# Context halves of the neighbourhood probabilities turned by DMA, values as half-precision pairs, low parts of the gated branches on VectorE: one core of a two-layer hybrid attention kernel

## The chip, the core and the metric

The kernel runs on one core of a Trainium2 chip. The core's engines work side by side: TensorE (PE) multiplies matrices and transposes by multiplying with an identity, VectorE (DVE) and ScalarE (ACT) work element by element, GpSimd (POOL) does so without reach into PSUM, and SyncE (SP) issues most of the DMAs. Each engine takes its instructions strictly in the order in which the program lists them. The metric is the device time of one execution in microseconds, the median of several runs; smaller is better.

## What is computed

Two layers of a trunk with two parallel attention branches on 512 latent tokens (8 rows of 64 columns) and 256 context tokens, width 1024, 8 heads of 64 channels per branch. Cut to what matters here:

```python
# branch A, per latent query: a window of 8 x 16 neighbours with a bias, and all 256 context keys, one softmax
s_win = einsum(qr, kw) * scale + bias[None]
s_ctx = einsum(qr, kc) * scale
p = softmax(concatenate([s_win, s_ctx]), axis=-1)
a_att = einsum(p[..., :128], vw) + einsum(p[..., 128:], vc)
# branch B: grouped queries (8 query heads, 2 key heads) over latent and context keys
b_att = attend(q, k_all, v_all)
# merge
o_a = (a_att * silu(a_z)) @ w_o_a
o_b = (b_att * silu(b_z)) @ w_o_b
out = (sigmoid(g_a) * o_a + sigmoid(g_b) * o_b) @ w_out
x = x + gate_x * out
```

In layer 0 the context tokens are queries as well (they attend to the context alone) and are updated in the same way; layer 1 returns the latent tokens.

## The kernel before

Everything is float32 in and out. A product of float32 matrices is made of three PE passes: each operand is split into a high part that PE takes at full speed and a low part, the rest (`mm3`, L433 to L435). Weights arrive by DMA on SP (`raw`, 3 buffers, L401 and L415), ACT casts the high part (`whi`, L403 and L418) and DVE or POOL subtracts for the low part (`wlo`, L406 and L420), with 8 buffers each.

A layer runs through these stages; times are those of the profiled execution.

1. Keys, values and queries of branch A. `evac_va` (L551) takes each of the six value tiles from PSUM: ACT writes the high part and DVE the low part, both float32, into two large tiles `va0` and `va1`.
2. The neighbourhood stage (160 to 295 us in layer 0, 768 to 882 us in layer 1): `pipeline` goes over the 8 heads, emits the scores of head h, then the values of head h-1, then a share of `fill`, the gate projections that have nothing to do with attention and keep PE at work. `na_scores` makes four score tiles of 128 queries by 512 keys: 256 window keys and the 256 context keys. For each, DVE adds the bias and finds the maximum (L958), ACT takes the exponential with its sum (L961), DVE inverts the sum (L762), and the tile is scaled, on DVE for two of the four (L765) and on POOL for the other two (L767, L768). `na_values` turns the probabilities so that keys lie on partitions: `transpose_split` lets PE transpose four 128 by 128 blocks into one PSUM tile (L777, L779), ACT copies the high part (L785) and DVE subtracts the low part (L786). A head takes four such rounds, two for the context half (used by L981, L982) and two for the window half (L986 to L992). In layer 0 the 256 context queries of a head take a fifth (`ctx_scores`, `ctx_values`, L905 and L906). `head_out` adds the two halves of the result (L795, L796) and multiplies it onto the gate (L797).
3. Keys, values and queries of branch B (295 to 385 us in layer 0).
4. The grouped-query stage (385 to 556 us, 940 to 1062 us). Here the probabilities are turned by DMA already: `turned` lets ACT write a 16-bit copy (L802) and DVE or POOL the 16-bit rest (L803), and one DMA on SP (L804) transposes both into `ht`. The values of this branch are 16-bit pairs, scaled to a known range by `shrink`, and `divide` puts the softmax sum and the scale back. While this stage runs, `prepare` splits branch A's gated result into high parts (`gah`, ACT, L656) and low parts (`gal`, POOL, L657), and `early` does so for three quarters of branch B's (`gbh`, `gbl`).
5. The output projections, the merge and the residual.

Large intermediate tiles come from one pool of nine (`big`). In layer 0 a background list (`gate_steps`) makes the output gate from `w_ada`: 8 weight tiles per half, each loaded by SP (L288) and multiplied with two vectors by DVE (L295). Half 0 runs beside the last heads of the neighbourhood stage, half 1 beside the grouped-query stage. The program is written head by head, and a list scheduler then fixes the order of the instructions on each engine; it decides which fill matmul stands between which parts of a head.

Of the kernel before, what the change touches and what calls it, by code (L numbers as in the profile page):

```python
# [7 lines left out]
F32 = mybir.dt.float32  # L8
# [17 lines left out]
NP_NA = (7, 8)  # L26
# [6 lines left out]
NA_POOL = (1, 3)  # L33
# [37 lines left out]
def hybrid_kernel(es: ExitStack, tc, x, ctx, cvec, w_ada, w_ada0, small, gvec, w_in, w_o_a, w_o_b, w_out,  # L71
# [482 lines left out]
    def split_v(ps, hi, lo, hi_src=None):  # L554
        S.copy(R(hi), ps)
        V.tensor_tensor(R(lo), ps, hi, ALU.subtract)

    def evac_va(dsts):
        def f(t, ps):
            d = dsts[t // 3].rearrange("p (t n) -> p t n", t=3)[:, t % 3, :]  # L560
            d = d.rearrange("p (r q d) -> p r q d", q=4, d=64)
            s = ps.rearrange("p (r e d) -> p r e d", e=2, d=64)
            hi, lo = d[:, :, 0:4:3, :], d[:, :, 1:3, :]
            split_v(s, hi, lo)
        return f
# [18 lines left out]
    def layer(l, hx, nxt, start):  # L584
# [144 lines left out]
        va = [big("va0"), big("va1")]  # L729
        w = load_w(W, C_AV, 512, KT, mix_lo)  # L730
        for t in range(6):
            tok_proj(w, 512, a_hx, t, evac_va(va))
# [16 lines left out]
        for t in range(qt):  # L749
            tok_proj(w, 512, a_hx, t, evac_na(qav, True, gq, YB if first else 4))  # L750
            run(bg, per_bg)
# [7 lines left out]
        if True:  # L759
            def softmax_tail(p, n, r, pieces, eng=None):  # L760

                V.reciprocal(r, r)  # L762
                for i, (c0, c1) in enumerate(pieces):
                    if eng is None:
                        V.tensor_scalar(p[:, c0:c1], p[:, c0:c1], r[:, i:i + 1], 0.5, ALU.mult, ALU.mult)  # L765
                    else:
                        G.tensor_scalar(r[:, i:i + 1], r[:, i:i + 1], 0.5, None, ALU.mult)  # L767
                        G.tensor_tensor(p[:, c0:c1], p[:, c0:c1],  # L768
                                        r[:, i:i + 1].to_broadcast([128, c1 - c0]), ALU.mult)

            def transpose_split(blocks, n0=0, n1=512):
# [8 lines left out]
                if att["spare"]:  # L780
                    hi, lo = R(p_tile()[:, 0:512]), R(p_tile()[:, 0:512])
                else:
                    hi = att["p"].tile([128, 512], F32R, tag="pth", name=nm("pth"), bufs=att["nt"])
                    lo = att["p"].tile([128, 512], F32R, tag="ptl", name=nm("ptl"), bufs=att["nt"])
# [715 lines left out]
```

## Time and profile before

| what | value |
|---|---|
| median of 3 runs | 1125.91 us (1125.44 to 1126.06) |
| profiled execution | 1127.56 us |
| its span, first to last instruction | 1125.6 us |
| mean granted PE clock | 0.993 |
| TensorE busy | 1093.3 us, 97% |
| VectorE busy | 774.7 us, 69% |
| ScalarE busy | 579.0 us, 51% |
| GpSimd busy | 490.6 us, 44% |

In a row of a stage table the pairs are busy microseconds and, in brackets, the number of instructions; PEld is the loading of weights into the array, which overlaps the matmuls; PEclk is the share of the clock that PE was granted. In a row of a group stand line, engine, operation, output and inputs with their shapes and the count, then busy microseconds and the mean nanoseconds of one, then the idle time just before and what ended it. In a row of the timeline stand start, duration, engine, line and operation, and in square brackets the idle time before it with its releaser. Matmul durations reach from issue to a modelled end and overlap one another; the distance between two starts is what one of them costs. A row for a tile or line gives the shortest, median and longest duration in nanoseconds.

### The profile page before, as it was taken

What the parts mean: (1) busy time and instruction counts of PE and PEld (TensorE: products, weight loads), DVE (VectorE), ACT (ScalarE), POOL (GpSimd) and SP (SyncE); (2) the same over time, 40 slices, a digit from 0 to 9 for tenths busy, and PEclk for the clock granted to TensorE, in tenths of its full rate; (3) what the DMA queues carried; (4) which work ended last, traced back from release to release, by engine and by line L of the source; (5) the groups of instructions that cost most, each with busy time, mean ns of one, the idle gap of its engine ahead of it and who ended that gap; (6) DMA issues with size and microseconds to landing.
All of it is one profiled execution on the core that took longest, in us unless ns stands there. A gap on an engine that the chain in (4) does not pass through costs nothing.

```text
span 1125.6 us, 16862 instructions
## 1 busy us (share of the span) xinstructions
PE 1093.3 (97%) x5826; PEld 905.3 (80%) x5826; DVE 774.7 (69%) x1492; ACT 579.0 (51%) x1154; POOL 490.6 (44%) x405
## 2 busy tenths in 40 slices
PE   8999999999999999979999999999999999999998
PEld 5688888888998877757788888888888987776677
DVE  4666788897466477776577785458878765677473
ACT  6453266665433576755330284326666446776431
POOL 1054254654247144454521545235554563563531
PEclk9999999999999999989999999999999999999999
DMA  9454322242351488869633532553333236989742
GB/s 373 143 172 140 114 63 66 73 136 89 93 168 38 123 201 185 185 172 269 173 108 125 183 129 72 142 174 92 100 107 116 59 105 172 188 224 239 197 145 80
DMA packets 192222, 161.29 MB, mean 143 GB/s; under 512 B 116364, under 2 KB 158088, under 8 KB 190472
## 3 DMA queue, kind: packets, MB, share of 16 engines
q1 hardware_dynamic: 184800, 145.82, 46.8%
q0 software_dynamic: 2368, 7.87, 2.1%
q10 hardware_dynamic: 4968, 6.53, 1.7%
q8 instruction: 46, 0.75, 0.3%
q14 instruction: 40, 0.33, 0.1%
HBM read 115.58 MB, written 17.32 MB: 118 GB/s over the span
## 4 chain that ended last, share of the span: by engine, by line
PE 38%; issue 4%; DVE 3%; DMA 3%; POOL 2%; ACT 1%; SPq 1%; POOLq 0%; ACTq 0%
PE psx L435 6%; PE psx L433 6%; PE psx L434 6%; PE psf L433 4%; PE psf L434 4%; PE psf L435 4%; PE pss L955 1%; PE pss L861 1%; POOL wlo L406 1%; PE pss L862 1%; PE pst L779 1%; PE pst L1148 1%; DMA raw<-in_w_o_a_dram 1%; PE pst L1149 1%; DMA raw<-in_w_in_dram 1%
## 5 line engine op out<-in xcount | busy, mean ns | idle before, releaser
L420 POOL TENSOR_TENSOR wlo<-raw,whi 128x512 fp32r<-128x512 f32 x70 | 97.9, 1405 | 106.1 <-ACT whi L418 70.4
L433 PE MATMUL psf<-hx,whi 128*128 128x512 f32 (+1 forms) x360 | 138.0, 383 | 3.2 <-ACT zt L614 2.4
L435 PE MATMUL psf<-hx,wlo 128*128 128x512 f32 (+1 forms) x360 | 135.8, 377 | 0.0
L434 PE MATMUL psf<-hx,whi 128*128 128x512 f32 (+1 forms) x360 | 135.1, 375 | 0.0
L433 PE MATMUL psx<-whi,hx 128*128 128x512 f32 (+1 forms) x328 | 120.8, 372 | 0.0
L434 PE MATMUL psx<-wlo,hx 128*128 128x512 f32 (+1 forms) x328 | 119.6, 366 | 0.0
L435 PE MATMUL psx<-whi,hx 128*128 128x512 f32 (+1 forms) x328 | 119.5, 365 | 0.0
L418 ACT CAST whi<-raw 128x512 fp32r<-128x512 f32 x136 | 82.3, 620 | 64.0 <-DMA raw<-in_w_in_dram 35.3
L406 POOL TENSOR_TENSOR wlo<-raw,whi 128x512 fp32r<-128x512 f32 x40 | 61.2, 1535 | 122.1 <-ACT whi L403 80.1
L803 POOL TENSOR_TENSOR h<-p,h 128x768 f16<-128x768 f32 (+1 forms) x40 | 65.7, 1644 | 96.4 <-ACT h L802 72.0
L403 ACT CAST whi<-raw 128x512 fp32r<-128x512 f32 x88 | 54.1, 623 | 99.2 <-PE psx L435 34.2
L420 DVE TENSOR_TENSOR wlo<-raw,whi 128x512 fp32r<-128x512 f32 x66 | 73.6, 1115 | 30.6 <-ACT whi L418 29.0
L504 POOL TENSOR_TENSOR ss<-ss,ehalf 128x8 f32<-128x8 f32 (+2 forms) x40 | 62.5, 1566 | 72.9 <-DVE ss L501 72.8
L433 PEld LDWEIGHTS psf<-hx,whi 128*128 128x128 f32 x360 | 67.9, 188 | 15.4 <-ACT zt L614 3.7
L435 PEld LDWEIGHTS psf<-hx,wlo 128*128 128x128 f32 x360 | 67.8, 188 | 11.6
L1131 DVE CUSTOM_DVE_ANT_0 p<-pss,vb 128x768 f32<-128x768 f32 x64 | 60.3, 953 | 23.6 <-PE pss L862 21.1
L434 PEld LDWEIGHTS psf<-hx,whi 128*128 128x128 f32 x360 | 67.9, 189 | 10.3
L1132 ACT ACTIVATE p<-pss,mx 128x768 f32<-128x768 f32 x64 | 57.6, 900 | 34.7 <-DVE mx L1131 33.7
L435 PEld LDWEIGHTS psx<-whi,hx 128*128 128x128 f32 x328 | 61.9, 189 | 10.0
L434 PEld LDWEIGHTS psx<-wlo,hx 128*128 128x128 f32 x328 | 62.0, 189 | 9.2
L433 PEld LDWEIGHTS psx<-whi,hx 128*128 128x128 f32 x328 | 61.8, 189 | 8.9
L435 PE MATMUL psx<-hx,wlo 128*128 128x256 f32 (+1 forms) x208 | 68.0, 327 | 0.0
(362 smaller groups left out, 3095.8 us busy)
## 6 DMA issues: line engine op xcount, KB each, us to landing
raw<-in_w_in_dram SPq DMA_DIRECT2D x168, 256.0 KB, 2.9
rawb<-in_w_ada_dram SPq DMA_DIRECT2D x48, 256.0 KB, 2.8
raw<-in_w_out_dram SPq DMA_DIRECT2D x32, 256.0 KB, 2.9
tg<-gs SPq DMA_DIRECT2D x4, 1536.0 KB, 6.8
rawx<-in_w_ada_dram SPq DMA_DIRECT2D x4, 1024.0 KB, 9.8
rawy<-in_w_ada_dram SPq DMA_DIRECT2D x4, 1024.0 KB, 9.5
gs<-zt ACTq DMA_DIRECT2D x16, 256.0 KB, 2.0
raw<-in_w_o_a_dram SPq DMA_DIRECT2D x16, 256.0 KB, 3.4
```

What stands on the lines that cost most here:

```text
L403: S.copy(hi[:, :n], raw[:, :n])
L406: e.tensor_tensor(lo[:, :n], raw[:, :n], F(hi[:, :n]), ALU.subtract)
L418: S.copy(hi, raw)
L420: lo_eng(i).tensor_tensor(lo, raw, F(hi), ALU.subtract)
L433: T.matmul(ps, lhs[0], rhs[0], start=first, stop=False)
L434: T.matmul(ps, lhs[0], rhs[1], start=False, stop=False)
L435: T.matmul(ps, lhs[1], rhs[0], start=False, stop=last)
L504: G.tensor_tensor(ss, ss, ehalf[:, :n], ALU.pow)
L779: T.transpose(pt[:, c0:c0 + 128], src, ident)
L803: eng.tensor_tensor(h[:, 1], p[:, :n], h[:, 0], ALU.subtract)
L1131: V.tensor_tensor_reduce(p, pss, lift, -1.0, 3e38, ALU.add, ALU.min, mx[:, 0:1])
L1132: S.activation(p, pss, AF.Exp, bias=mx[:, 0:1], accum_out=r[:, i:i + 1])
```

## The change

**Values of branch A.** `evac_va` now only copies the tile to float32 (`vf`), takes absolute values on ACT and their maximum on DVE. `split_va`, after the first query tile, finds the largest maximum (`shrink`, with one transposition and one small matmul on PE), and `halves` writes scaled 16-bit pairs in three passes on ACT and three on DVE. `head_out` multiplies the scale back in its two existing operations.

**Context half.** The two context rounds of `transpose_split` in `na_values` go. `na_scores` calls `turned` for each tile's 256 context columns: an ACT cast, a POOL subtraction and a DMA transposition (two, of 64 partitions each, for the edge tile), which land in `ht`, one more large tile with a half for even and one for odd heads. In layer 0 the context queries go the same way (`hc`, 512 columns). The context matmuls come first in a head's accumulation, so a head's values begin when its transpositions have landed.

**Scaling.** The two tiles that POOL scaled are scaled by ACT, after one more DVE multiplication of the 128 inverted sums.

**Window half.** Still transposed on PE; both parts are now 16-bit, side by side in one tile.

**Low parts of the gated branches.** `prepare` and `early` give `hilo` DVE in place of POOL.

**Other places.** Half 0 of layer 0's `gate_steps` moves from the neighbourhood stage to stage 3. Branch B's values keep two slots instead of three, and their size is found by absolute values. Layer 0 gets 8 probability buffers instead of 7.

```diff
-NP_NA = (7, 8)
+NP_NA = (8, 8)
+NH_NA = 4
-NA_POOL = (1, 3)
+NA_ACT = (1, 3)
+P_UP = 2.0 ** 14
...
+    def size(v, junk, mx):
+        S.activation(junk, v, AF.Abs)
+        V.tensor_reduce(mx, junk, AX, ALU.max)
...
+    def halves(v, d, s):
+        S.activation(d[:, :, 0, :], v, AF.Copy, scale=s)
+        V.scalar_tensor_tensor(d[:, :, 1, :], v, s, d[:, :, 0, :], ALU.mult, ALU.subtract)
...
-            hilo(za, gated["a"], range(4))
+            hilo(za, gated["a"], range(4), V)
...
+        def evac_va(t, ps):
+            S.copy(vf[:, t, :], ps)
+            size(ps, vab[:, 512 * t:512 * t + 512], vmx[:, t:t + 1])
+        def split_va():
+            V.tensor_reduce(vmx[:, 6:7], vmx[:, 0:6], AX, ALU.max)
+            shrink(vmx[:, 6:7], vsa, vsa[0:1, 2:3], 0.5 / P_UP)
+            for t in range(0, 6, 2):
+                halves(vf[:, t:t + 2, :].rearrange("p t (h d) -> p (t h) d", d=64),
+                       va[:, t:t + 2].rearrange("p t h q d -> p (t h) q d"), vsa[:, 0:1])
...
+                if on_act:
+                    V.tensor_scalar(r, r, P_UP, None, ALU.mult)
                 for i, (c0, c1) in enumerate(pieces):
-                    if eng is None:
-                        V.tensor_scalar(p[:, c0:c1], p[:, c0:c1], r[:, i:i + 1], 0.5, ALU.mult, ALU.mult)
+                    if on_act:
+                        S.activation(p[:, c0:c1], p[:, c0:c1], AF.Copy, scale=r[:, i:i + 1])
                     else:
-                        G.tensor_scalar(r[:, i:i + 1], r[:, i:i + 1], 0.5, None, ALU.mult)
-                        G.tensor_tensor(p[:, c0:c1], p[:, c0:c1],
-                                        r[:, i:i + 1].to_broadcast([128, c1 - c0]), ALU.mult)
+                        V.tensor_scalar(p[:, c0:c1], p[:, c0:c1], r[:, i:i + 1], P_UP, ALU.mult, ALU.mult)
...
+            turns = big("ht").bitcast(F16)
...
+                    at = [(0, 64, 0), (448, 512, 64)] if i == 0 else [(128 * i - 64, 128 * i + 64, 0)]
+                    turned(p[:, 256:512], 256, [(ht[:, :, a:b], n, n + b - a) for a, b, n in at], G)
...
                 for k in range(2):
-                    c0 = 256 + 128 * k
-                    hi, lo = transpose_split(
-                        [(pe[:, c0:c0 + 128], None)]
-                        + [(pp[:, c0:c0 + 128], 64 + 128 * i) for i, pp in enumerate((p0, p1, p2))])
-                    T.matmul(po, vsl(4 + k), hi, start=k == 0, stop=False)
-                    T.matmul(po, vsl(4 + k), lo, start=False, stop=False)
+                    for a in range(2):
+                        T.matmul(po, vsl(4 + k), ht[:, 2 * a + k, :], start=k + a == 0, stop=False)
...
-            bg = gate_steps((0,), att["p"]) if first else []
-            pipeline(fill, 9, na_first, values_of(za, na_values), bg=bg)
+            bg = []
+            pipeline(fill, 9, na_first, values_of(za, na_values, vsa[:, 1:2], False), bg=bg)
...
-            bg = []
+            bg = gate_steps((0,), hp["p"]) if first else []
             w = load_w2(W, C_BKV, KT, mix_lo)
...
-                hilo(zb, gated["b"], range(3))
+                hilo(zb, gated["b"], range(3), V)
```

What the scheduler makes of it is seen in the order of the instructions. On PE, the values of layer 0's first neighbourhood head (`psv`; `pth` and `ptl` are the turned context halves, `pst` the PSUM tiles of the window's transposes) stood before the change so:

```order
L982 MATMUL psv_1671<-ptl_1678,va_116_712 128x512
L981 MATMUL psv_1671<-pth_1688,va_116_712 128x512
L777 MATMUL pst_1694<-ident,p_1473 128x2x64
L779 MATMUL pst_1694<-ident,p_1483 128x128 x2
L982 MATMUL psv_1671<-ptl_1689,va_116_712 128x512
L779 MATMUL pst_1694<-ident,p_1494 128x128
L777 MATMUL pst_1707<-ident,p_1473 128x2x64
L779 MATMUL pst_1707<-ident,p_1494 128x128
L779 MATMUL pst_1707<-ident,p_1504 128x128 x2
```

and now, at the same place, the context matmuls read what the DMA turned (`ht`), behind the first scores of the next head (L972), and the window's parts (`pt`) follow; the weights of 16-bit matmuls are listed as rows of their own:

```order
L972 MATMUL pss_1885<-kh_1476,qs_1862 128x512
L972 MATMUL pss_1885<-kl_1477,qs_1862 128x512
L996 LDWEIGHTS va_712
L996 MATMUL psv_1736<-ht_1475,va_712 128x512
L996 LDWEIGHTS va_712
L996 MATMUL psv_1736<-ht_1475,va_712 128x512
L996 LDWEIGHTS va_712
L996 MATMUL psv_1736<-ht_1475,va_712 128x512
L996 LDWEIGHTS va_712
L996 MATMUL psv_1736<-ht_1475,va_712 128x512
L1000 LDWEIGHTS va_712
L1000 MATMUL psv_1736<-pt_1746,va_712 128x192
```

The four context matmuls now stand together, with no transpose of their own before them.

On POOL, in layer 0's grouped-query stage, the low parts of branch A (`gal`) stood before the change as one row of four between two weight subtractions:

```order
L797 TENSOR_TENSOR zb_4086<-zb_4086,ho_5477 64x512
L420 TENSOR_TENSOR wlo_5512<-raw_5508,whi_5510 128x512
L657 TENSOR_TENSOR gal_5328<-za_1045,gah_5327 128x768 x4
L420 TENSOR_TENSOR wlo_5690<-raw_5686,whi_5688 128x512
L797 TENSOR_TENSOR zb_4086<-zb_4086,ho_5490 64x256
```

and now they stand on DVE (L666), among a later head's work (L897 is a score maximum, L848 the multiplication by the inverted sums, L1147 the next head's first maximum):

```order
L823 TENSOR_TENSOR ho_5434<-pst_5421,ho_5434 64x512
L666 TENSOR_TENSOR gal_5285<-za_1053,gah_5284 128x768
L897 TENSOR_REDUCE mx_5403<-pss_5398 128x2
L666 TENSOR_TENSOR gal_5285<-za_1053,gah_5284 128x768 x2
L899 TENSOR_SCALAR mx_5403<-mx_5403 128x2
L848 SCALAR_TENSOR_TENSOR zb_4043<-pst_5592,vb_3395,zb_4043 64x512
L666 TENSOR_TENSOR gal_5285<-za_1053,gah_5284 128x768
L422 TENSOR_TENSOR wlo_5475<-raw_5471,whi_5473 128x512
L1147 ISA p_5529,mx_5530<-pss_5524,vb_3395 128x768
```

The train of four left POOL and is spread over DVE's row with two or three instructions of the heads between its parts.

On SP, in layer 0's neighbourhood stage, weights (`raw`), gate weights (`rawb`) and bias tiles (`bint`, `bedg`) followed each other before the change:

```order
L935 DMA bedg_1448<-in_bias_edge_dram 64x128 x2
L415 DMA raw_2716<-in_w_in_dram 128x2x256
L288 DMA rawb_2589<-in_w_ada_dram 128x512
L933 DMA bint_1447<-in_bias_int_dram 128x256
L415 DMA raw_2722<-in_w_in_dram 128x2x256
L415 DMA raw_2988<-in_w_in_dram 128x2x256
```

and now weights and bias tiles share the queue with the transpositions (L840):

```order
L417 DMA raw_2298<-in_w_in_dram 128x2x256
L840 DMA_TRANSPOSE ht_1475<-h_1896 128x4x128
L840 DMA_TRANSPOSE ht_1475<-h_1910 128x4x128
L840 DMA_TRANSPOSE ht_1475<-hc_1943 128x8x128
L840 DMA_TRANSPOSE ht_1475<-h_1925 128x4x128
L840 DMA_TRANSPOSE ht_1475<-h_2119 128x4x64 x2
L840 DMA_TRANSPOSE ht_1475<-h_2135 128x4x128
L947 DMA bint_1469<-in_bias_int_dram 128x256
L949 DMA bedg_1470<-in_bias_edge_dram 64x128 x2
```

A head brings six transpositions to this queue in layer 0 and five in layer 1, and a bias or weight load behind one of them waits for the cast and the subtraction that it waits for.

More of the change, by code (lines that the diff above doesn't have):

```diff
@@ L552, in evac_na, with shrink @@
         return f
[L554 to L565, printed above, removed]
+    def size(v, junk, mx):
+        S.activation(junk, v, AF.Abs)
+        V.tensor_reduce(mx, junk, AX, ALU.max)
+    def shrink(mx, s, row, post):
+        pt = psw(512, "t")
+        T.transpose(pt[0:1, 0:128], mx, ident)
+        V.tensor_reduce(row, pt[0:1, 0:128], AX, ALU.max)
+        T.matmul(pt[:, 128:129], row.to_broadcast([1, 128]), ident[0:1, 0:1], start=True, stop=True)
+        V.tensor_scalar(s[:, 1:2], pt[:, 128:129], 1.0e-30, 1.0 / V_UP, ALU.max, ALU.mult)
+        V.reciprocal(s[:, 0:1], s[:, 1:2])
+        V.tensor_scalar(s[:, 1:2], s[:, 1:2], post, None, ALU.mult)
+    def halves(v, d, s):
+        S.activation(d[:, :, 0, :], v, AF.Copy, scale=s)
+        V.scalar_tensor_tensor(d[:, :, 1, :], v, s, d[:, :, 0, :], ALU.mult, ALU.subtract)
     def rope_heads(npair, ps, rs, ta, tb, dst, t):
@@ L865, in cut, with ctx_scores @@
                 return lambda k: k[:, a:b]
[L867 removed]
+            def ctx_scores(q, kh, kl, ct, late=True):
                 pss = ps_score()
```

138 lines of the change are left out of this document (67 added, 71 removed).

## The prediction

> **What bounds the kernel now.** I read the engine totals first, then the busy time by stage, then the waits and the timeline where TensorE (PE) stands still.
>
> ```profile
> PE 1093.3 (97%) x5826; PEld 905.3 (80%) x5826; DVE 774.7 (69%) x1492; ACT 579.0 (51%) x1154; POOL 490.6 (44%) x405
> ```
> ```profile
> core 0: us, PE busy (x) PEld busy (x) DVE busy (x) ACT busy (x) POOL busy (x), PEclk, DMA share, GB/s
> 160.00:295.00 135.00, 135.00 (x857) 120.90 (x856) 110.14 (x245) 84.98 (x193) 68.93 (x68) 1.00 0.28 88
> 385.00:480.00 95.00, 90.53 (x523) 74.45 (x522) 70.09 (x136) 66.35 (x131) 41.51 (x29) 1.00 0.83 181
> 489.00:507.00 18.00, 9.98 (x36) 7.58 (x35) 15.63 (x13) 8.73 (x19) 12.76 (x10) 0.72 0.69 218
> 768.00:882.00 114.00, 112.52 (x613) 96.21 (x612) 97.39 (x187) 74.12 (x155) 61.00 (x59) 1.00 0.32 99
> 940.00:1000.00 60.00, 58.45 (x280) 45.72 (x279) 39.46 (x66) 45.08 (x82) 27.68 (x19) 1.00 0.85 182
> 1000.00:1052.00 52.00, 48.65 (x227) 34.66 (x225) 39.12 (x61) 36.67 (x66) 31.28 (x21) 1.00 1.07 251
> ```
> The first column pair of each row is the length of the stretch and PE's busy time in it. 160 to 295 us and 768 to 882 us are the two neighbourhood stages: PE is busy for 135.00 of 135 and 112.52 of 114 us, and no other engine is above 85%. There PE work is time. The grouped-query stages (385, 940 and 1000 us) leave PE idle for 3 to 6%. At 489 to 507 us PE does 9.98 of 18 us at a granted clock of 0.72: the one hole worth naming.
>
> **Part A: transposes leave PE.** Per head the eight context transposes go (16 heads: 128), and in layer 0 four more for the context queries (8 heads: 32). That is 160 of 288, or 40 groups of four.
>
> ```profile
> 867.94 0.27 PE L777 MATMUL pst<-ident,p 128*128 128x128 f32 x1
> 868.05 0.49 PE L779 MATMUL pst<-ident,p 128*128 128x128 f32 x3
> 868.29 0.36 PE L433 MATMUL psf<-whi,hx 128*128 128x256 f32 x1
> 868.49 0.28 PE L434 MATMUL psf<-wlo,hx 128*128 128x256 f32 x1
> 868.61 0.28 PE L435 MATMUL psf<-whi,hx 128*128 128x256 f32 x1
> ```
> Durations overlap, so I take distances between starts. From the group's start to the second matmul behind it are 868.49 - 867.94 = 0.55 us; one ordinary 256-column step (868.61 - 868.49 = 0.12) belongs to the matmul, so a group costs 0.43 us. 40 x 0.43 = **-17.2 us**.
>
> **Part B: half-precision value matmuls.**
>
> ```profile
> 188.22 0.40 PE L982 MATMUL psv<-ptl,va 128*128 128x512 f32 x1
> 188.46 0.40 PE L981 MATMUL psv<-pth,va 128*128 128x512 f32 x1
> ...
> 1002.91 0.38 PE L1149 MATMUL pst<-ht,vb 128*128 128x512 f16 x1
> 1003.13 0.38 PE L1148 MATMUL pst<-ht,vb 128*128 128x512 f16 x1
> 1003.34 0.38 PE L1149 MATMUL pst<-ht,vb 128*128 128x512 f16 x1
> ```
> The same size steps at 0.24 us in the neighbourhood branch and at 0.215 us with 16-bit operands. 64 such matmuls save 64 x 0.02 = 1.3 us; the narrower ones should add some. I take **-2 us**, between 0 (they step as before) and -3.
>
> **Part C: the hole at 489 us.** In layer 0 the gated branch's four low parts run on GpSimd (POOL) in one train.
>
> ```profile
> 492.20 8.26 DVE L420 TENSOR_TENSOR wlo<-raw,whi 128x512 fp32r<-128x512 f32 x1
> ...
> L420 DVE TENSOR_TENSOR wlo<-raw,whi 128x512 fp32r<-128x512 f32 x66 | 73.6, 1115 | 30.6 <-ACT whi L418 29.0 <-PE psf L435 1.0
> ...
> 491.54 7.15 POOL L657 TENSOR_TENSOR gal<-za,gah 128x768 fp32r<-128x768 f32 x4
> ...
> 502.15 0.69 PE L811 MATMUL psv<-ident,r 128*128 128x128 f32 x2 [5.80 <-DVE ho L796]
> ```
> ```profile
> PE psf L434 <- POOL gbl L657: 1.0, 1, 1.0
> ...
> PE psf L434 <- POOL gal L657: 0.6, 1, 0.6
> ```
> VectorE (DVE) starts one weight subtraction at 492.20 and is held 8.26 us, where its group's mean is 1.1. Queued behind it are the query staging, the reciprocal and the head's addition, whose result frees the PSUM tile that PE waits for: 5.80 us. PE also waits 0.6 us for the low part itself, and the lost clock is 18 x (1 - 0.72) = 5.0 us. The hole is worth 11.4 us. The change takes the train off POOL. What is late next is DVE: four subtractions of 768 columns, whose nearest row is
>
> ```profile
> L803 DVE TENSOR_TENSOR h<-p,h x32: 947/959/2072, 387.6 to 1046.8; 128x768 f16<-128x768 f32 x32
> ```
> so 3.8 us of DVE, with a score maximum and a multiplication set among them in the new order. I charge two thirds, 2.4 us: **-9 us**, between -11.4 and 0 (DVE's own train stalls PE as long). Layer 1's wait of 1.0 us for POOL's low parts (gbl) should go too: **-1 us**.
>
> The Trainium skill ("SBUF — State Buffer", section "SBUF: two separate sides") says that a two-input DVE operation and a GpSimd operation exclude each other for one whole instruction. The trace differs in size: DVE stayed out through the train and the POOL instruction after it, not for one of some 1.8 us. By the rule alone the subtraction would end near 494.7, the train would not be the hole's cause, and part C would be 0 instead of -9; that is rival 2.
>
> **Part D: what takes the transposes' place.** ScalarE (ACT) casts and GpSimd subtractions make 16-bit pairs, and the SP queue issues DMA transposes.
>
> ```profile
> L382 ACT CAST hx<-yT 128x256 fp32r<-128x256 f32 x21 | 8.0, 406 | 8.7 <-DVE yT L380 8.7
> L418 ACT CAST whi<-raw 128x512 fp32r<-128x512 f32 x136 | 82.3, 620 | 64.0 <-DMA raw<-in_w_in_dram 35.3 <-DMA raw<-in_w_o_a_dram 8.6 <-PE psf L434 6.7
> L785 ACT CAST pth<-pst 128x512 fp32r<-128x512 f32 x35 | 19.7, 585 | 6.5 <-PE pst L779 4.8 <-PE psv L905 1.4
> L786 DVE TENSOR_TENSOR ptl<-pst,pth 128x512 fp32r<-128x512 f32 x35 | 23.4, 682 | 3.1 <-ACT pth L785 2.9
> L768 POOL TENSOR_TENSOR p<-p,r 128x512 f32<-128x512 f32 x32 | 35.0, 1093 | 2.7
> L803 POOL TENSOR_TENSOR h<-p,h 128x768 f16<-128x768 f32 x32 | 56.0, 1750 | 89.7 <-ACT h L802 70.1 <-issue 13.8 <-PE psf L435 5.1
> L803 POOL TENSOR_TENSOR h<-p,h 128x512 f16<-128x512 f32 x8 | 9.8, 1219 | 6.7 <-issue 4.7 <-ACT h L802 1.9
> ```
> ACT per head: four casts of 256 columns (4 x 0.406), two scalings that POOL did (2 x 0.62), less two PSUM copies (2 x 0.585) = +1.7 us; in layer 0 another 0.62 comes and another 0.585 goes. Over 8 heads +13.6 us each: 88 of some 105 us in layer 1 (84%), 99 of some 125 in layer 0. DVE loses two or three subtractions of 0.682 per head, -11 and -16 us. POOL swaps two scalings of 1.1 for four subtractions of 256 columns, near 0.69 by the step from 512 to 768: about even, +10 us in layer 0 for the context pair. All stay below PE, but ACT now waits in order for DVE's reciprocal before its scaling, and behind it stand the copies that free PE's two fill tiles. The value matmuls wait for a DMA of the head before, a head's time of slack (13 to 15 us); only the last head has less, with some 38 fill matmuls of 0.23 us and two heads' values between. So PE will not stay at 100%. Bounds: 0 (all hidden) and the worst grouped-query stretch, 48.65/52, which is 6.4% of some 229 us = 14.7. The stretch at 940 us has the same transposes at three times the size and is 97.4% busy: 6 us, less the 1.5 idle today. I take **+5 us**.
>
> **Costed at almost nothing.**
>
> ```profile
> 60.00:160.00 100.00, 100.00 (x495) 83.93 (x494) 71.50 (x142) 42.72 (x76) 43.97 (x26) 1.00 0.43 127
> ...
> L295 DVE CUSTOM_DVE_ANT_0 rawb<-rawb,cb 128x512 f32<-128x512 f32 x56 | 41.3, 740 | 10.0 <-DMA rawb<-in_w_ada_dram 8.4 <-DMA cb<-cd 1.1
> ...
> 295.00:385.00 90.00, 90.00 (x527) 78.91 (x526) 47.22 (x83) 34.14 (x69) 38.98 (x31) 1.00 0.33 103
> ```
> The value stage (layer 0's lies within 60 to 160 us) gains six absolute-value passes, three scaling passes and a scale search; ACT is 43% busy under a PE that never stops. Uncovered, the six passes would be 3.6 us a layer; I add **+0.5 us** for PE's two small search steps. Layer 0's 16 gate dot products, their loads and SP issues move to 295 to 385 us, where DVE is busy 47 of 90 us; uncovered they would cost 12 us (16 x 0.74).
>
> **Sum**: -17.2 - 2 - 9 - 1 + 5 + 0.5 = -23.7 us. The profiled execution took 1127.56 us (span 1125.6), 1.65 above the median of the runs, 1125.91. On that median the forecast is 1125.91 - 23.7 = **1102 us**.
>
> **Rivals.**
>
> 1. ACT or the DMA wait sets the pace of the neighbourhood stages, and PE idles as in the worst grouped-query stretch: 14.7 instead of 5, so **1112 us**. For it: 84% on ACT and 82% on DVE, both in order. Against: a score tile there is freed by DVE, not by ACT, and has three buffers.
> 2. Part C gives nothing, since DVE's train blocks as POOL's did: **1111 us**.
> 3. The SP queue becomes the bound, and the kernel is **slower**. It issues one thing after another:
>
> ```profile
> L804 SPq DMA_TRANSPOSE ht<-h x64: 1274/1678/7132, 388.6 to 1051.1; - x64
> ...
> L804 SPq DMA_TRANSPOSE ct<-h x4: 1233/1726/6013, 417.4 to 542.4; - x4
> ```
> ```profile
> L935 SPq DMA_DIRECT2D bedg<-in_bias_edge_dram x32: 465/580/621, 135.6 to 857.4; - x32
> ```
> Twelve blocks take 1.68 us and eight 1.73 (medians), so four may take as long. A head issues six in layer 0, five in layer 1, beside two bias pieces of 0.58 and, by the same row as an upper price, three or four other loads: 3 us. At 1.68 us that is 13.1 of 15.6 us and 11.4 of 13.1. The point is (13.1 - 3)/5 = 2.0 us a transpose; above it weights, biases and transposes queue behind each other. At 2.7 us the heads take 16.5 and 19.2 us: +18 us in layer 1, +19 in layer 0, less C and its 1 us: **1153 us**. Against: the medians come from transposes two to three times the size, in stretches where the DMA engines are over 80% taken.
>
> The Trainium skill ("DMA: Bandwidth & Descriptors", section "Why a DMA increments its semaphore by 16 and not by 1") says of chips before trn3 that such a transpose is pushed tile by tile. By that a third of the size takes a third of the issue, some 0.56 us, and this rival falls away; the rows at eight and twelve blocks do not show it.
>
> 4. Gain and new stalls cancel, within 0.2% (2.3 us, about what a measurement of this kernel tells from no change): **1126 us**.
>
> **How the numbers follow.** Forecast 0.46, rival 1 0.20, rival 2 0.17, rival 3 0.12, rival 4 0.05. Faster is 0.46 + 0.20 + 0.17 = 0.83, same 0.05, slower 0.12. Low end: B at -3, C at -11.4 and D at 0 give 1125.9 - 17.2 - 3 - 11.4 - 1 + 0.5 = 1093.8; I set 1092. The high end takes in rivals 1 and 2 together (14.7 and no C: 1121): 1122.
>
> **What would show it.** PE should have 160 fewer 128-column transposes, and 16-bit value matmuls stepping 0.215 us; the rows L996 and L919 of the new code carry them. In the neighbourhood stages PE should stay above 96% busy, with ACT near 84%. Around 480 us no DVE subtraction should take 8 us and the granted clock should stay 1.00. If a transpose's issue on SP takes above 2 us, or PE waits for the turned tiles by the microsecond per head, the forecast is wrong; if PE's holes merely move to where DVE makes the low parts, part C is.

## The result, and the profile after

The changed kernel takes 1125.54 us (median of 20 runs, 1120.92 to 1129.61), the kernel before 1126.29 us (20 runs beside it). The ratio is 0.9993 with a 95% interval of 0.9983 to 1.0003: no difference that can be measured. The forecast was 1102 us; the outcome was rival 4, to which 0.05 was given. The profiled execution took 1127.07 us, its span is 1125.3.

The engine totals of the changed kernel come first, then the same two neighbourhood stages, the hole and the grouped-query stretches as in the prediction.

```profile
PE 1080.6 (96%) x5672; PEld 876.5 (78%) x5672; DVE 767.2 (68%) x1510; ACT 617.9 (55%) x1236; POOL 477.1 (42%) x399
```
```profile
160.00:295.00 135.00, 130.92 (x792) 110.75 (x791) 96.42 (x210) 99.01 (x225) 72.90 (x76) 0.97 0.54 128
385.00:480.00 95.00, 90.21 (x512) 73.66 (x511) 70.42 (x133) 63.85 (x126) 43.17 (x30) 1.00 0.80 178
489.00:507.00 18.00, 13.98 (x69) 9.84 (x70) 15.45 (x24) 10.19 (x20) 6.65 (x5) 1.00 0.97 287
768.00:882.00 114.00, 106.73 (x545) 82.40 (x544) 88.59 (x196) 89.30 (x191) 63.95 (x58) 1.00 0.51 129
```

The reader is to see three things. PE has less to do. The hole at 489 us is half filled (13.98 us of work in 18, at full clock, where 9.98 stood). And the neighbourhood stages, where PE had been idle for 0 and 1.5 us, now leave it idle for 4.1 and 7.3 us, although ScalarE (ACT) is only 73% and 78% busy and VectorE (DVE) 71% and 78%.

For a balance without the overlap of matmuls I take, for every PE instruction, the distance to the next start. Its work is this distance up to the median of its form; what lies beyond is lost time, waits and halved clock together (excesses below some 0.04 us are counted as work). The first matmul behind a group of probability transposes starts its successor some 0.087 us late (the median; 75 groups before, 30 after), which I count as the group's work. **Work falls from 1056.8 to 1037.0 us, 19.8 less**, where the prediction had 17.2 + 2 - 0.5 = 18.7. Sorting the forms more finely or more coarsely moves the totals by several us, and the fall to between 20 and 21 us. The lost time, by stretches:

| stretch, us | lost before | lost after |
|---|---|---|
| 0 to 150 | 16.4 | 16.5 |
| 150 to 300, neighbourhood, layer 0 | 0.1 | 9.1 |
| 300 to 480 | 9.3 | 10.5 |
| 480 to 520, the hole | 14.5 | 7.0 |
| 520 to 565, end of the grouped queries | 4.4 | 11.3 |
| 565 to 690, merge and change of layer | 1.3 | 4.7 |
| 690 to 770 | 0.8 | 1.0 |
| 770 to 885, neighbourhood, layer 1 | 2.6 | 11.2 |
| 885 to the end | 13.8 | 11.4 |
| sum (of the unrounded rows) | 63.2 | 82.6 |

So 19.8 us of work went and 19.4 us of lost time came; the spans differ by 0.3. Four rows gained 3 us or more of lost time: both neighbourhood stages (+9.0, +8.6), the end of the grouped queries (+6.9) and the change of layer (+3.4). The hole lost 7.5. These are single executions; among versions that share the code of the hole, its row differs by up to 3 us.

PE's waits in the changed kernel show who is named there, in layer 0's neighbourhood stage, from 480 to 560 us, and at the change of layer:

```profile
PE pst L805 <- DVE p L795: 3.2, 1, 3.2
```
```profile
PE pst L1164 <- DMA ht<-h: 2.5, 1, 2.5
PE psf L435 <- DVE tg L701: 2.0, 3, 1.1
PE psf L436 <- DVE gal L666: 1.8, 2, 0.9
PE psx L460 <- DVE ho L823: 1.7, 1, 1.7
```
```profile
PE psx L436 <- DVE wlo L408: 1.0, 1, 1.0
PE pst L343 <- ACT half L346: 0.8, 2, 0.6
```

The 6-us wait for `ho` in the hole is gone. In its place PE waits shortly for the low parts (`gal`). Later it waits for the last head's turned probabilities (`ht`), for that head's `ho`, and at the change of layer for layer 1's scaled input (`half`) and for the low part of a weight (`wlo`).

### The profile page after: what moved, and what is told of

It reads as the page before. It is cut to its first block, busy times and chain, and to the rows that moved or that the text cites. A ratio compares the mean times of both kernels' runs of the same rounds, so it can differ in the third digit from the quotient of the medians.

```text
span 1125.3 us, 16869 instructions
## 1 busy us (share of the span) xinstructions
PE 1080.6 (96%) x5672; PEld 876.5 (78%) x5672; DVE 767.2 (68%) x1510; ACT 617.9 (55%) x1236; POOL 477.1 (42%) x399
## 5 line engine op out<-in xcount | busy, mean ns | idle before, releaser
L836 POOL TENSOR_TENSOR h<-p,h 128x256 f16<-128x256 f32 (+2 forms) x104 | 112.8, 1093 | 148.9 <-ACT h L835 97.5
L422 DVE TENSOR_TENSOR wlo<-raw,whi 128x512 fp32r<-128x512 f32 x66 | 60.4, 915 | 39.1 <-ACT whi L420 37.0
L835 ACT CAST h<-p 128x256 f16<-128x256 f32 (+2 forms) x136 | 81.4, 617 | 9.2 <-POOL wlo L422 5.3
L1147 DVE CUSTOM_DVE_ANT_0 p<-pss,vb 128x768 f32<-128x768 f32 x64 | 60.2, 952 | 23.6 <-PE pss L885 21.2
L436 PEld LDWEIGHTS psf<-hx,whi 128*128 128x128 f32 x360 | 67.9, 189 | 10.5
L436 PEld LDWEIGHTS psx<-wlo,hx 128*128 128x128 f32 x328 | 62.0, 189 | 11.4 <-DVE wlo L408 1.4
```

The lines of the kernel that those rows point to most:

```text
L422: lo_eng(i).tensor_tensor(lo, raw, F(hi), ALU.subtract)
L436: T.matmul(ps, lhs[0], rhs[1], start=False, stop=False)
L835: S.copy(h[:, 0], p[:, :n])
L836: eng.tensor_tensor(h[:, 1], p[:, :n], h[:, 0], ALU.subtract)
L1147: V.tensor_tensor_reduce(p, pss, lift, -1.0, 3e38, ALU.add, ALU.min, mx[:, 0:1])
```

## The experiments: part C

**C alone, and C undone.** In the kernel before, and the other way round in the changed kernel:

```diff
-            hilo(za, gated["a"], range(4))
+            hilo(za, gated["a"], range(4), V)
...
-                hilo(zb, gated["b"], range(3))
+                hilo(zb, gated["b"], range(3), V)
```

> The kernel before with part C alone (low parts of both gated branches on VectorE). Theory 'given back': the hole at 489 to 507 us shrinks, but the end of layer 0's grouped-query stage then waits for the last heads' own chain (cast, subtraction, transposition), so the time stays within 3 us of before: 1123 to 1127 us. Rival, the forecast's part C: 8 to 10 us less, 1116 to 1118 us.

Measured: 1129.24 us, ratio to the kernel before 1.0019 (1.0009 to 1.0028), 2 us slower.

> The changed kernel with part C undone (low parts of the gated branches on GpSimd again). Theory 'given back': within 3 us of the changed kernel, 1123 to 1129 us. Rival, the forecast's part C: 8 to 10 us more, 1133 to 1136 us.

Measured: 1123.58 us, ratio 0.9968 (0.9955 to 0.9981); the changed kernel without C is faster than with it. Both go against the forecast's -9. C alone misses my new expectation on the far side, C undone lies at the low end of it: C did not just give back, it cost 2 to 3 us. The lost time of C alone is 8.4 us at 480 to 520 us (14.5 before), 6.3 at 520 to 565 (4.4) and 5.9 from 565 to 690 (1.3): 6.1 us gained, 6.5 lost later. At the change of layer the waits of C alone name ACT's `half`, the scaled input of layer 1:

```profile
PE pst L341 <- ACT half L344: 1.6, 2, 1.4
```

**Branch B's half of C.** The loss at 520 to 565 us has another cause, which lies in C itself. In the changed kernel DVE makes branch B's low parts (`gbl`) there in one train of four, and `ho`, the result that PE waits for, stands behind it (DVE first, then PE):

```profile
541.50 4.36 DVE L666 TENSOR_TENSOR gbl<-zb,gbh 128x768 fp32r<-128x768 f32 x4
545.89 0.43 DVE L823 TENSOR_TENSOR ho<-psv,ho 64x256 f32<-64x256 f32 x1
```
```profile
546.37 0.50 PE L460 MATMUL psx<-gbh,whi 128*128 128x512 f32 x1 [1.75 <-DVE ho L823]
```

C alone has the same wait; in the kernel before, with these low parts on POOL, it is 0.3 us. The versions of the changed kernel that follow bear it out: by the same balance the five with branch B's low parts on POOL lose 4.1 to 8.1 us in this stretch, the eleven with them on DVE 9.2 to 11.9 (before: 4.4). A changed kernel in which only this half is undone was not run.

**The second chain.** `half` needs layer 1's modulation (`modc`). Its weights (`rawb`, 16 tiles in two buffers) are loaded through POOL's queue and multiplied by DVE from the output projection on. Here is the end of that chain in the changed kernel, on DVE and ACT:

```profile
652.26 0.18 DVE L242 TENSOR_TENSOR modc<-modc,g 128x16 f32<-128x16 f32 x1
...
653.01 2.89 ACT L346 ACTIVATE half<-pst,modc 128x128 f32<-128x128 f32 x8
```

and in the kernel before:

```profile
649.75 0.17 DVE L240 TENSOR_TENSOR modc<-modc,g 128x16 f32<-128x16 f32 x1
...
650.46 2.89 ACT L344 ACTIVATE half<-pst,modc 128x128 f32<-128x128 f32 x8
```

The first transposes of layer 1's input stand at 643.55 us after and 646.90 before: PE comes 3.4 us earlier, and the chain ends 2.5 us later. The test starts the chain at the merge of branch B:

```diff
+            bg = ada_steps(1, range(16), (1,), 2, mp, G) + [lambda: ada_mod(1)] if first else []
+            run(bg, 1)
             chunks = o_chunks("b", None, evac_b)
...
                 for piece in chunks[i][1]:
                     piece()
+                    run(bg, 1)
...
-            bg = ada_steps(1, range(16), (1,), 2, mp, G) + [lambda: ada_mod(1)] if first else []
-            run(bg, 1)
```

> The changed kernel with the 16 weight tiles of layer 1's modulation loaded and multiplied from the merge of branch B on, instead of from the output projection on. Theory 'second chain': PE's wait at the layer change (3.5 us idle from 654 to 660 us) comes from this chain, which ends at 652.26 us and does not move when PE is earlier; it goes: 1122 to 1123 us. Rival: the wait is that of the first weights and high parts there, and stays: 1125 to 1126 us.

Measured: 1120.20 us, ratio 0.9949 (0.9930 to 0.9969). `modc` is made at 642.08 us, before the first transposes at 648.33 (PE is later by then in this execution), and PE is busy through the whole change of layer:

```profile
642.08 0.17 DVE L242 TENSOR_TENSOR modc<-modc,g 128x16 f32<-128x16 f32 x1
```
```profile
640.00:690.00 50.00, 47.73 (x228) 37.88 (x227) 37.26 (x70) 29.93 (x72) 20.59 (x24) 1.00 0.35 116
640.00:690.00 50.00, 50.00 (x245) 41.48 (x244) 35.79 (x62) 30.70 (x72) 18.55 (x23) 1.00 0.31 103
```

The first row of the second fence is the stretch in the changed kernel, with 2.3 us idle; the row below it is the run with the early chain, 50.00 of 50. So the wait at the change of layer was the chain's. The lost time from 565 to 690 us falls by 3.8 us in the profiled execution; the time falls by some 5 us, below the 1122 to 1123 us that I expected, and what the rest is was not followed up.

**Whose gain is it?** The same edit in the kernel before with C, and without C:

> The kernel before with part C and with layer 1's modulation chain started at the merge. Theory 'given back': C alone lost 4.6 us more at the layer change; with the chain out of the way the same C is 0.1 to 0.4% faster than before, 1122 to 1125 us. Rival: C's loss lies elsewhere, and this stays 0.2% slower, 1129 us.

Measured: 1124.17 us, ratio 0.9972 (0.9960 to 0.9985).

> The kernel before with only the modulation chain started at the merge. Theory 'given back': PE idles 1.3 us at the layer change there, so at most 1 us is to be had, 1125.5 to 1127 us, and the step from 1129.2 to 1124.2 us between C alone and C with the early chain is C's own gain. Rival: 3 us or more less by itself, 1121 to 1124 us; then C gives nothing even so.

Measured: 1129.02 us, ratio 1.0018 (1.0007 to 1.0030). Here is the clearest result of these runs: C alone +0.19%, the early chain alone +0.18%, both together -0.28%. Alone the early chain brings nothing, since PE lost only 1.3 us there in the kernel before (why it costs 2 us I can't say). With the chain early, C takes 1129.0 to 1124.2 us, some 5 us, and the profiled executions agree: 7.1 us less lost in the hole, 2.6 more at 520 to 565 us. So C has a gain of its own. In the changed kernel it was taken at two later places: against the run with C undone the hole loses 7.1 us less, the end of the grouped queries 6.2 us more and the change of layer 2.7 us more.

## The experiments: part D

**DVE held by POOL.** The largest stall of layer 0's neighbourhood stage, in the changed kernel: DVE, then POOL.

```profile
177.69 4.41 DVE L795 TENSOR_SCALAR p<-p,r 128x256 f32<-128x256 f32 x3
...
185.67 3.31 DVE L878 TENSOR_TENSOR qs<-qa,qs 64x768 fp32r<-64x768 f32 x1
189.01 0.49 DVE L795 TENSOR_SCALAR p<-p,r 128x512 f32<-128x512 f32 x1
```
```profile
177.85 1.59 POOL L827 TENSOR_TENSOR za<-za,ho 64x512 f32<-64x512 f32 x1 [3.00 <-ACT pt L811]
179.40 1.17 POOL L836 TENSOR_TENSOR hc<-p,hc 128x512 f16<-128x512 f32 x1
180.53 1.28 POOL L422 TENSOR_TENSOR wlo<-raw,whi 128x512 fp32r<-128x512 f32 x1
...
185.11 1.83 POOL L868 TENSOR_TENSOR kl<-ka,kh 64x768 fp32r<-64x768 f32 x1 [1.77 <-PE psf L437]
186.90 1.27 POOL L422 TENSOR_TENSOR wlo<-raw,whi 128x512 fp32r<-128x512 f32 x1
```

Three scalings take 4.41 us and end at 182.10 (the last alone takes 3.88, where the scaling at 189.01 takes 0.49), just behind a POOL train that ends at 181.81; a query subtraction takes 3.31 us and ends at 188.98, 0.8 behind a train that ends at 188.17. PE waits until 189.56 for the scaling behind it. The clock follows in these stretches of the changed kernel:

```profile
185.00:190.00 5.00, 1.77 (x10) 1.24 (x9) 4.94 (x5) 4.93 (x14) 3.06 (x2) 0.88 0.22 50
190.00:195.00 5.00, 4.42 (x19) 2.97 (x18) 4.96 (x14) 3.65 (x9) 4.05 (x5) 0.50 0.47 124
```

If this is what part D costs, it should go when DVE makes the low parts itself:

```diff
-                    turned(p[:, 256:512], 256, [(ht[:, :, a:b], n, n + b - a) for a, b, n in at], G)
+                    turned(p[:, 256:512], 256, [(ht[:, :, a:b], n, n + b - a) for a, b, n in at], V)
```

> The changed kernel with the 16-bit low parts of the neighbourhood context on VectorE instead of GpSimd (four subtractions of 256 columns a head; the context queries' one stays). Theory 'held VectorE': the stalls of the neighbourhood stages come from VectorE operations that stay out through trains of GpSimd (4.41 us at 177.69, 3.31 at 185.67, 3.58 at 861.24); with two thirds of those trains gone PE's idle time there falls by 6 to 12 us, 1114 to 1120 us. Rival, pace: VectorE and ScalarE are simply too busy, four more subtractions of some 0.4 us a head make it 0 to 5 us slower, 1125 to 1131 us.

Measured: 1123.83 us, ratio 0.9976 (0.9966 to 0.9985), 2 us less than the changed kernel. The stall above is gone, but the lost time of the two neighbourhood stages only falls from 20.3 to 16.2 us. The hold is a part of it, not most of it; the theory falls as the main cause, as far as this run can tell: DVE now also has the four subtractions of a head to do, and this run doesn't part the two effects.

**Which piece of the new work.** Next I left pieces out for heads 1 to 7 of each layer (and for their context queries), whose context matmuls then read head 0's tile. Only the main line of each edit is shown.

```diff
-                    turned(p[:, 256:512], 256, [(ht[:, :, a:b], n, n + b - a) for a, b, n in at], G)
+                    turned(p[:, 256:512], 256, [(ht[:, :, a:b], n, n + b - a) for a, b, n in at] if h == 0 else [], G)
```

> The changed kernel without the DMA transpositions of heads 1 to 7 in the neighbourhood stages: casts and subtractions stay, the context matmuls of all heads read head 0's turned tile, so the result leaves those heads' context out. Theory 'SP and landing': what part D costs (6 us in layer 0, 7 in layer 1 by PE's idle time) is due to the SP queue and to the wait for the turned tiles: 8 to 11 us less than the changed kernel, 1114 to 1117 us. Theory 'pair work': it is due to the casts and subtractions on ScalarE and GpSimd: at most 3 us less, 1122 to 1125 us.

Measured: 1128.83 us, ratio 1.0009 (0.9995 to 1.0022). Without the transpositions nothing is gained; the time lies above both expectations. The next run leaves out the casts and subtractions of these heads too.

> As the run before, and the casts and subtractions of heads 1 to 7 are left out too. Both theories: PE's idle time in the neighbourhood stages goes back to that of the kernel before, 10 to 13 us less than the changed kernel, 1112 to 1115 us; by 'pair work' most of this step lies between this run and the run before, by 'SP and landing' almost none. Rival: the time stays above 1120 us, then part D is not what took the gain.

Measured: 1112.98 us, ratio 0.9871 (0.9854 to 0.9888). Without the pair work the two stages lose 6.1 us, against 20.3 in the changed kernel, and PE is busy throughout the first:

```profile
150.00:300.00 150.00, 150.00 (x932) 129.65 (x932) 101.17 (x241) 99.03 (x216) 54.05 (x49) 1.00 0.33 98
770.00:885.00 115.00, 112.61 (x642) 92.71 (x641) 86.16 (x217) 84.21 (x178) 48.40 (x41) 1.00 0.37 107
```

In the sum the SP queue and the landing of the turned tiles are not what costs (without them layer 1's stage loses 2.6 us less, layer 0's 4.1 more); casts and subtractions carry the cost. Then each of the two alone, still without the transpositions; the edit shown leaves the subtractions out, its counterpart leaves the casts out and subtracts the tile from itself:

```diff
                 S.copy(h[:, 0], p[:, :n])
-                eng.tensor_tensor(h[:, 1], p[:, :n], h[:, 0], ALU.subtract)
+                if out != []:
+                    eng.tensor_tensor(h[:, 1], p[:, :n], h[:, 0], ALU.subtract)
```

> The changed kernel without transpositions and without the 16-bit subtractions of heads 1 to 7 in the neighbourhood stages; ScalarE's casts stay (those heads' context is left out of the result). Theory 'held VectorE': GpSimd's subtractions are what costs, by holding VectorE; without them the time is near that without pairs, 1113 to 1117 us. Rival 'ScalarE pace': the casts cost, 1122 to 1129 us. If both share it: 1118 to 1121 us.

Measured: 1115.57 us, ratio 0.9900 (0.9877 to 0.9923).

> The counterpart: transpositions and ScalarE's casts of heads 1 to 7 left out, GpSimd's subtractions kept (of the tile from itself, the same size; those heads' context is left out of the result). Theory 'held VectorE': near the changed kernel, 1122 to 1129 us. Rival 'ScalarE pace': near the run without pairs, 1113 to 1117 us. If both share it: 1118 to 1121 us.

Measured: 1114.46 us, ratio 0.9895 (0.9874 to 0.9915). Neither theory fits both: each piece alone costs some 3 us. In the run with casts alone ACT is as busy as in the changed kernel, and PE hardly stops; in the run with subtractions alone POOL is:

```profile
150.00:300.00 150.00, 148.19 (x913) 126.36 (x913) 98.45 (x240) 109.09 (x247) 52.95 (x47) 1.00 0.33 96
```
```profile
150.00:300.00 150.00, 149.14 (x920) 127.98 (x919) 103.25 (x240) 97.66 (x213) 80.75 (x83) 1.00 0.33 96
```

against the changed kernel's 145.92 of PE, 106.72 of ACT and 80.22 of POOL in the same stretch. **Both pieces, without the wait between them**, is the next case:

```diff
-                eng.tensor_tensor(h[:, 1], p[:, :n], h[:, 0], ALU.subtract)
+                eng.tensor_tensor(h[:, 1], p[:, :n], h[:, 0] if out != [] else p[:, :n], ALU.subtract)
```

> The run without transpositions (1128.8 us) with casts and subtractions both kept, at the same sizes, but the subtraction no longer reads the cast's result (it takes the tile from itself), so GpSimd doesn't wait for ScalarE's cast; those heads' context is left out of the result. Theory 'coupling' (GpSimd waiting in order behind ScalarE's cast, which waits for VectorE's scaling, which GpSimd's next operations hold): 1112 to 1118 us, as without one of the two. Rival 'sum of loads' (either engine can bear its own part, not both): 1125 to 1131 us.

Measured: 1120.21 us, ratio 0.9938 (0.9922 to 0.9953): between the two expectations. Of the 15.5 us between the runs without pairs and without transpositions (0.9871 and 1.0009 of 1126.5 us), 8.0 belong to the dependence of the subtraction on the cast (1.0009 - 0.9938), and 7.5 to having both at all. Each of these differences is uncertain by some 2 us, so the 7.5 are not clear of the 6.0 that the two cost alone, added up (3.3 + 2.7): what goes beyond the sum of the two pieces is the dependence. The lost time of the two neighbourhood stages goes the same way: 6.1 us without pairs, 8.7 with casts alone, 9.2 with subtractions alone, 16.0 with both uncoupled, 21.9 with both coupled.

**Relief and other forms.** With `NA_ACT = ()` all tiles are scaled on DVE; with the scaling on ACT left out altogether nothing takes its place:

```diff
-                    if on_act:
-                        S.activation(p[:, c0:c1], p[:, c0:c1], AF.Copy, scale=r[:, i:i + 1])
-                    else:
+                    if not on_act:
```

> The changed kernel with all four tiles of a head scaled on VectorE, none on ScalarE (1.24 us a head less on ScalarE, 1 us more on VectorE). 'ScalarE pace': 3 to 6 us less than the changed kernel, 1119 to 1122 us. 'Held VectorE': two more scalings a head that GpSimd can hold (4.41 us where 1.2 was due), 2 to 5 us more, 1127 to 1130 us.

Measured: 1127.97 us, ratio 1.0012 (1.0000 to 1.0024): no gain, but some 2 us more than the changed kernel.

> The changed kernel without ScalarE's scaling of two tiles a head (these tiles stay unscaled, the result is left wrong by it): 1.4 us a head less on ScalarE, nothing added elsewhere, casts, subtractions and transpositions as they are. Theory 'sum of loads': any relief of an engine in the chain takes idle time off PE, 5 to 10 us less than the changed kernel, 1115 to 1120 us. Rival: only the pairs' own dependence costs, 1123 to 1126 us.

Measured: 1130.43 us, ratio 1.0029 (1.0013 to 1.0045), slower with less work, against both expectations. In layer 1's stage of this run DVE waits for bias tiles, and PE for DVE:

```profile
DVE p L973 <- DMA bedg<-in_bias_edge_dram: 11.5, 2, 7.7
```
```profile
PE pss L882 <- DVE mx L973: 3.1, 1, 3.1
```

The bias loads stand on SP behind transpositions that wait for their pairs. The changed kernel has one such wait (5.1 us of DVE, at 857.49 us), the kernel before none. Last, the pairs straight from the unscaled probabilities, so that the cast needs no scaling by DVE and POOL has no part:

```diff
+                        S.activation(h[:, 0, cs], p[:, cs], AF.Copy, scale=r[:, i:i + 1])
+                        V.scalar_tensor_tensor(h[:, 1, cs], p[:, cs], r[:, i:i + 1], h[:, 0, cs],
+                                               ALU.mult, ALU.subtract)
```

> The changed kernel with the context pairs made straight from the unscaled probabilities: ScalarE writes the scaled 16-bit part in its cast, VectorE makes the rest in one operation with the same scale (0.4 us, four a head), and only the window half is scaled in place. The cast no longer waits for VectorE's scaling, and GpSimd has no part in it. Theory 'coupling': PE's idle time in the neighbourhood stages falls by 8 to 12 us, 1113 to 1117 us. Rival: VectorE waits for the cast in its place, as where it made the low parts: 1121 to 1125 us.

Measured: 1125.04 us, ratio 0.9974 (0.9962 to 0.9986). Only 2 us, the rival's time. The 16-bit rest still waits for the cast here, on DVE in place of POOL, so the dependence inside the pair stays; taking the scaling and POOL out of the chain is not enough.

## The experiments: joined versions

> The changed kernel with the modulation chain at the merge, the neighbourhood low parts on VectorE, and branch B's early low parts on GpSimd again. If the stalls are separate, their gains add: 3.7 + 4.3 + 2 us less than the changed kernel, 1115 to 1116 us. Rival: each gain is taken by the next wait, 1119 to 1121 us.

Measured: 1119.47 us, ratio 0.9934 (0.9918 to 0.9949): the early chain, the low parts on DVE and branch B's on POOL give 6 to 7 us together, where 10 were due if they added. (Versions of different groups are compared by their ratios to the kernel before, which was timed beside each group.)

> The joined kernel (1119.5 us) with the low parts of two of the four tiles on GpSimd again. If VectorE's load (83% in the neighbourhood stages there) is what is left, 1 to 3 us less, 1116 to 1118 us; if each GpSimd subtraction brings its hold of VectorE back, 1 to 3 us more, 1120 to 1122 us.

Measured: 1121.02 us, ratio 0.9957 (0.9943 to 0.9971): some 2.6 us more by the ratios, at the edge of what these runs can tell.

> The joined kernel (1119.5 us) with the pairs made directly. 'Coupling': 6 to 9 us less, 1110 to 1113 us. Rival: 1117 to 1120 us.

Measured: 1119.62 us, ratio 0.9932 (0.9917 to 0.9946), the same as the joined kernel.

> The joined kernel (1119.5 us) with branch A's low parts on GpSimd too, so that nothing of part C's main pieces is left. If C is worth something once the later chains are out of its way: 2 to 4 us more, 1121.5 to 1123.5 us. Rival, C is worth nothing even then: 1119 to 1120 us.

Measured: 1124.09 us, ratio 0.9969 (0.9957 to 0.9981). Branch A's low parts on DVE are worth some 4 us in the joined kernel (0.9969 - 0.9934): this half of part C gains, once its successors are out of the way and branch B's half is back on POOL. The joined kernel, at 0.993, beats both the kernel before and the changed one.

## Why the prediction was wrong, step by step

**Part A was right, B too small.** The transposes gave 12.9 us by their own distances (25.5 to 12.6) and 4.3 by the matmuls behind their groups (6.6 to 2.3): 17.2, as forecast. The value matmuls, the context queries' included, gave 4.3 us where 2 was forecast, since the narrow ones of the window gained more in all than the wide ones; 1.7 us of small differences go against it. The context matmuls step 0.2175 us each (four from 866.92 to 867.79, on PE of the changed kernel):

```profile
866.92 1.04 PE L996 MATMUL pss<-ht,va 128*128 128x512 f16 x4 [1.05 <-DMA ht<-h]
867.79 0.27 PE L803 MATMUL pss<-ident,p 128*128 128x128 f32 x1
```

**Part C failed at "what is late next".** The term was -9 and came to nothing. The hole was sized rightly (11.4 us, of which the change took 7.5). But the step named only DVE as late next, and DVE alone in the hole itself. The next ones stood 40 and 160 us further on: the end of the grouped queries at 520 to 565 us (+6.9 us), where the `gbl` train that C itself put on DVE holds `ho` back and the last head's turned probabilities are waited for, and the modulation chain (+3.4 us), which ends at 652 us though PE comes earlier. The views of before hardly show them as waits (0.6 us for `ht`, 0.3 for `ho`), since PE came just late enough. The prediction's own sign, holes that move to where DVE makes the low parts, came true in part. The charge for DVE's own train was right in kind: in the changed kernel the `gal` train is held in its turn,

```profile
487.87 4.63 DVE L666 TENSOR_TENSOR gal<-za,gah 128x768 fp32r<-128x768 f32 x2
488.44 3.24 POOL L422 TENSOR_TENSOR wlo<-raw,whi 128x512 fp32r<-128x512 f32 x2
```

the two rows being DVE's and POOL's, and PE waits 1.8 us for it. The -1 for layer 1 came to little: PE waits 0.7 us for DVE's `gbl` there, where it waited 1.0 for POOL's.

**Part D was mis-sized**: +5 forecast, with 14.7 as the far bound; the neighbourhood stages lost 17.6 us more, the largest miss of the sum. The loads were right (ACT 99.01 and 89.30 us in the stage rows, 99 and 88 forecast). The inference failed: that engines below 85% leave PE's idle time at that of the grouped-query stretches, and that the worst of those is a bound. Casts alone keep ACT at 109.09 of 150 us and cost 3 us, and less load on ACT gains nothing. What the runs show in its place is the pair work: some 6 us for casts and subtractions by themselves, and 8 us for the wait of the subtraction for the cast. That this wait reaches PE through three engines, each strictly in order, that pass every tile on to one another, is argued and not shown.

**The rivals.** Rival 1 had nearly the right size for part D (14.7 for 17.6), and half the mechanism: it named ACT or the DMA wait, and the run without transpositions shows no gain from taking the DMA wait away. Rival 2 had the right time for part C and a part of the cause: DVE's train does hold PE, by 1.8 us for `gal` in the hole and by 1.7 behind `gbl`. It did not name the last head's turned probabilities or the modulation chain, which took the rest. Both together were the high end, 1121 us; the change of layer (3.4 us) and part D's excess over its bound (2.9) came on top, and 2.3 more for part B went the other way, so the range was too narrow. Rival 4 had the time; that gains and losses cancelled to within 0.3 us is luck, as no step of it says why they should. Rival 3 falls as the bound: an SP transposition of four blocks takes 1.22 us here (median, 160 to 295 us), below its point of 2.0. Over the whole kernel:

```profile
L840 SPq DMA_TRANSPOSE ht<-h x144: 1174/1272/7891, 158.3 to 1051.2; - x144
```

The Trainium skill ("DMA: Bandwidth & Descriptors", section "Why a DMA increments its semaphore by 16 and not by 1") says that before trn3 a transposition is pushed tile by tile. An issue of four blocks at 1.17 us at least, against 1.23 for eight and 1.27 for twelve in the rows of before, shows no such proportion here; the 0.56 us worked out from it was wrong.

**What stays open.** The sizes of the pair work add up: some 14 us in all, about 3 for either half, about 8 for their dependence. How the dependence reaches PE is not settled: the runs that shorten the chain (low parts on DVE, direct pairs) gain 2 us each, and leaving out the transpositions or ACT's scaling gains nothing. Why the last head's turned probabilities come late at 531 us, and why the early chain alone costs 2 us, is open too. Each edit also makes the scheduler set the order of all later instructions anew, and each version has its holes in other places; a run with a changed edit and an unchanged order was not made.

## What to carry to other kernels

Where PE is busy 97% of the time, work taken off PE is worth its time only as far as the chains of the other engines have slack: look for every chain that ends just before PE reaches its result (before the change ACT's `half`, which needs `modc`, ended at 653.35 us, and PE's next transposes of that input stood at 653.31), not only for those that PE waits for now. Look also for what the moved work itself now stands in front of, at every place where it was moved: one half of part C gained some 4 us, the other held PE up. A stall that is removed should be tried together with the next chain moved forward; each alone looked like a loss here (+0.19% and +0.18%), and together they gained 0.28%. The busy share of an engine that works in order says little about whether one more cast in a chain of three engines is free.

## What the runs showed of the hardware

The issue of a DMA transposition on SP takes at least 1.17, 1.23 and 1.27 us for four, eight and twelve blocks (shortest rows of the two kernels): small ones are hardly cheaper for the queue. DVE operations with SBUF operands stayed out not for one POOL instruction but for a whole back-to-back train (4.41 us beside 4.0 us of POOL, 3.31 beside 3.1), as in the hole of the kernel before. After a PE stall of 3.2 us the granted clock was 0.50 from 190 to 195 us of the changed kernel; by my estimate from these two figures that is up to 2.5 us more lost.
